# Rows of late stores shared unevenly among DMAs: from SyncE's queue to GpSimd's

## The chip, the cores and the metric

The kernel runs on one core of one Trainium2 chip. The metric is the device time of one execution in microseconds; of several runs the median is given. All times of the profile are from one execution that the hardware profiler recorded.

## The reference

For 8 batches of 12 heads, 512 positions and 64 dimensions, attention under a tree mask: position i sees itself and its ancestors (parent of i is (i-1)//2).

```python
mask = np.zeros((seq, seq))
for i in range(seq):
    mask[i, i] = 1
    parent = i
    while parent > 0:
        parent = (parent - 1) // 2
        mask[i, parent] = 1
scores = np.einsum('bhqd,bhkd->bhqk', Q, K) * scale + (1 - mask) * (-1e9)
weights = np.exp(scores - np.max(scores, axis=-1, keepdims=True))
weights = weights / (np.sum(weights, axis=-1, keepdims=True) + 1e-10)
return np.einsum('bhqk,bhkd->bhqd', weights, V).astype(np.float32)
```

Q, K, V and the output are float32, 12.58 MB each.

## The kernel before

The 96 heads are numbered through, two to a step, so there are 48 steps; from step 8 on two steps share a block of four heads, and `head(i, a)` gives the head of step i. A head's 512 positions lie on 128 partitions with four positions each, so a head is 1 KB of float32 on each partition.

All bulk loads are issued by GpSimd (POOL) and turn float32 into bfloat16 on the way; only the first two heads of Q and K come through SyncE (SP) and ScalarE. Per step, TensorE transposes K and Q, makes two sets of scores with the mask added as a product of code words, ScalarE takes the exponential into `e1` and `e2`, TensorE multiplies by the values with a column of ones, and VectorE (`norm`, lines 581 and 583) divides by the sum and writes the result into `of`, a float32 tile of 128 partitions for a group of eight heads. There are 11 such tiles in turn for the 12 groups.

Stores go out group by group. `store(eng, h0, n, step, p0, p1)` (line 590) issues one DMA on the queue of `eng` for n heads from h0 and for the partitions (rows) p0 to p1. The order on POOL is a list that `pool_program` writes out: loads, copies of V (`spread_pool`, `spread_top`) and stores. `pool(i)`, called at the end of each step, issues from the front of the list as long as `ready` says that what the front needs has been made. So an entry that is not ready holds back all behind it. In the loop over the last loads the store of group g is entered once the loads are BEHIND = 56 heads further; that places groups 0 to 4. What remains, groups 5 to 10, stands behind the last load and the last copies, with group 9 (heads 72 to 79) cut to its first four heads:

```python
for g in range(stored, NH // VO - 1):
    ops.append((store, nc.gpsimd, VO * g, APART - VO * g if g == APART // VO else VO))
```

Heads 76 to 79 are stored by `store_apart` in step 41 on SyncE's queue, in four DMAs over rows 0 to 63, 64 to 90, 91 to 115 and 116 to 127. Group 11 (heads 88 to 95) is stored in pieces, on SyncE's queue in the last three steps and, after the last step, one head each on SyncE's and ScalarE's queue.

Of the kernel before, what the change touches and what calls it, by code (L numbers as in the profile page):

```python
# [119 lines left out]
def kernel(  # L120
# [7 lines left out]
    nc = tc.nc  # L128
    B, H, S, D = Q.shape
    P = nc.NUM_PARTITIONS  # L130
    assert S == 512 and D == 64 and P == 128 and (B * H) % 4 == 0
    scale = float(1.0 / np.sqrt(D))
    NH = B * H
# [3 lines left out]
    KB, VB, VO = 8, 16, 8  # L137
# [126 lines left out]
    def head(i, a):  # L264

        return 2 * i + a if i < WIDE else 4 * (i // 2) + i % 2 + 2 * a
# [187 lines left out]
    def scores1(i):  # L454

        sp = psS.tile([P, 2, 512], fp32, name="s1")
        for a in range(2):
            nc.tensor.matmul(  # L458
                out=sp[:, a, :],
                lhsT=(k1code if i < WIDE else k1wide)[64 * a:64 * a + CODE_ROWS, :],  # L460
                rhs=(q1code[64 * a:64 * a + CODE_ROWS, :] if i < WIDE
                     else q1wide[64 * a:64 * a + CODE_ROWS, :, :]),
                start=True, stop=False,
            )
        for a in range(2):
            nc.tensor.matmul(  # L466
                out=sp[:, a, :], lhsT=keys(i, a, TOP),
                rhs=qTs[i][64 * a:64 * a + 64, :, :].rearrange("p t c -> p (t c)"),
                start=False, stop=True,
            )  # L470
        et = etpool.tile([P, 2, 4, 128], bf16, name="e1")
        nc.scalar.activation(  # L472
            out=et[:, :, :, :].rearrange("p a t c -> p (a t c)"),
            in_=sp[:, :, :].rearrange("p a c -> p (a c)"),
            func=AF.Exp, scale=scale,
        ) if i < WIDE else nc.scalar.activation(  # L476
            out=et[:, :, :, :].rearrange("p a t (r u) -> p a (t r) u", u=2),
            in_=sp[:, :, :].rearrange("p a (u c) -> p a c u", u=2),
            func=AF.Exp, scale=scale,
        )  # L480
        ets[i] = et
# [92 lines left out]
    def norm(i):  # L574
        g = head(i, 0) // VO
        if g not in ofs:
            ofs[g] = opool.tile([P, VO, 4, D], fp32, name="of")
        o4 = obs[i][:, :, 0:260].rearrange("p a (t c) -> p a t c", c=D + 1)
        rec = small.tile([P, 2, 4, 1], fp32, name="rec")
        for a, n in ((0, 2),) if i < NP - 1 else ((0, 1), (1, 1)):  # L580
            nc.vector.reciprocal(out=rec[:, a:a + n, :, :], in_=o4[:, a:a + n, :, D:D + 1])  # L581
            first, last, step = head(i, a) % VO, head(i, a + n - 1) % VO, head(i, 1) - head(i, 0)
            nc.vector.tensor_tensor(  # L583
                out=ofs[g][:, first:last + 1:step, :, :],
                in0=o4[:, a:a + n, :, 0:D],
                in1=rec[:, a:a + n, :, :].to_broadcast([P, n, 4, D]),
                op=ALU.mult,
            )

    def store(eng, h0, n, step=1, p0=0, p1=P):  # L590
        g, f = divmod(h0, VO)
        return eng.dma_start(  # L592
            out=Or[p0:p1, h0:h0 + step * (n - 1) + 1:step, :],
            in_=ofs[g][p0:p1, f:f + step * (n - 1) + 1:step, :, :].rearrange(
                "p h t d -> p h (t d)"
            ),
        )

    APART, APART_AT, APART_ROWS = 76, 41, (0, 64, 91, 116, P)

    def store_apart():

        for p0, p1 in zip(APART_ROWS, APART_ROWS[1:]):
            store(nc.sync, APART, 4, 1, p0, p1)

    def pool_program():

        ops = [
            (load_k, 2, 2), (load_q, 2, 2), (load_v, 0, 4), (load_v, 4, 4),
            (load_k, 4, 2), (load_k, 6, 2), (load_q, 4, 2), (load_k, 8, 4),  # L610
            (load_q, 6, 2), (load_q, 8, 4), (load_v, 8, 8), (load_k, 12, 4),
            (load_q, 12, 4), (load_k, 16, 4), (load_rows, 1, "upper"),
            (load_q, 16, 4), (load_rows, 1, "even"), (load_k, 20, 4), (load_rows, 1, "odd"),
            (load_q, 20, 4), (load_k, 24, 8), (load_q, 24, 4), (load_rows, 2, "upper"),
            (load_q, 28, 4), (load_k, 32, 4), (load_rows, 2, "even", "odd"),
            (load_q, 32, 8), (load_k, 36, 4), (load_rows, 3, "upper"),
            (spread_pool, (1, "Z0", 8, 16), (1, "Z1", 8, 16)),
            (load_k, 40, 8), (load_q, 40, 8), (load_rows, 3, "even", "odd"),
            (spread_top, 2, 0, 16), (spread_pool, (2, "Z0", 0, 16), (2, "Z1", 0, 16)),
            (load_q, 48, 4), (spread_pool, (2, "X", 0, 8)),  # L620
            (load_k, 48, 8), (spread_pool, (2, "X", 8, 16)),
            (load_q, 52, 4), (load_rows, 4, "upper"), (spread_top, 3, 0, 16),
            (load_k, 56, 8), (load_q, 56, 8), (load_rows, 4, "even", "odd"),
            (spread_pool, (3, "X", 0, 8), (3, "Z0", 0, 16), (3, "Z1", 0, 16), (3, "X", 8, 16)),
            (load_rows, 5, "upper"), (store, nc.gpsimd, 0, VO),
        ]
        loaded, stored = 88, 1
        for h in range(64, NH, KB):
            top = [(spread_top, h // VB + 0)] if h % VB == 8 and 4 <= h // VB + 0 < NH // VB else []
            ops += [(load_k, h, KB)] + top + [(load_q, h, KB)]  # L630
            while loaded < min(h + 32, NH):
                names = ("even", "odd") if loaded % VB else ("upper",)
                ops.append((load_rows, loaded // VB) + names)
                loaded += KB
            if top:
                o = h // VB
                ops.append((spread_pool, (o, "X", 0, 16), (o, "Z0", 0, 16), (o, "Z1", 0, 16)))
            while VO * stored + VO + BEHIND <= h + KB:
                ops.append((store, nc.gpsimd, VO * stored, VO))
                stored += 1  # L640
        for g in range(stored, NH // VO - 1):
            ops.append((store, nc.gpsimd, VO * g, APART - VO * g if g == APART // VO else VO))
        return ops

    def ready(op, i):

        f, args = op[0], op[1:]
        if f in (load_k, load_q):
            return 2 * (i + 3) >= args[0] + args[1] - 4 * KB
        if f is load_v:  # L650
            return True
        if f is load_rows:
            return 2 * i >= VB * (args[0] - 2)
        if f is spread_pool:
            tops = [(("vt", "M", VB * o + h) in issued) for o, part, h0, h1 in args if part == "X"
                    for h in range(h0, h1)]
            return 2 * i >= VB * (args[0][0] + 1 - NV) and all(tops)
        if f is spread_top:
            return 2 * i >= VB * (args[0] + 1 - NV)
        return 2 * i >= args[1] + args[2]  # L660

    BY_VECTOR = {
        0: [(0, 2, 0, 8), (0, 7, 0, 4), (0, 1, 0, 8), (0, 6, 0, 8), (0, 3, 0, 8), (0, 9, 0, 8)],
# [44 lines left out]
    def pool(i):  # L708
        while program and ready(program[0], i):
            op = program.pop(0)  # L710
            op[0](*op[1:])
# [18 lines left out]
    for i in range(NP + 1):  # L730
        steps = FIRST[i] if i < len(FIRST) else "SVK" if i % 2 else "SVQ"
        for step in steps:
            if step == "S" and i < NP:
                scores1(i)
                scores2(i)
            if step == "V" and i >= 1:
                values(i - 1)
                norm(i - 1)
                valued = True
            if step == "K" and kdone < NP:  # L740
                kdone = turn("kst", kdone)
            if step == "Q" and qdone < NP:
                qdone = turn("qst", qdone)
            if step == "W":
                nc.scalar.copy(
                    out=codes[64:64 + CODE_ROWS, 1280:1536], in_=codes[0:CODE_ROWS, 1280:1536]
                )
            if step == "X":
                spin("s1" if valued else "ob", 2)
            if step == "D":  # L750
                spread_by(nc.vector.tensor_copy, BY_VECTOR, STEADY_VECTOR, i)
            if step == "A":
                spread_by(nc.scalar.copy, BY_SCALAR, {}, i)
        if "D" not in steps:
            spread_by(nc.vector.tensor_copy, BY_VECTOR, STEADY_VECTOR, i)
        if "A" not in steps:
            spread_by(nc.scalar.copy, BY_SCALAR, {}, i)
        pool(i)
        if i == APART_AT:
            store_apart()  # L760
        if i >= NP - 3 and i < NP:
            store(nc.sync, head(i - 1, 0), 2, 2)
    assert not program
# [32 lines left out]
```

## Time and profile before

| | |
|---|---|
| runs | 134.94 us median of 3 (134.68 to 135.85) |
| profiled execution | 134.27 us, its span 132.4 us |
| busy in the span | PE 113.4, DVE 100.1, ACT 94.4, POOL 72.9 us |
| HBM | 37.94 MB read, 12.58 MB written |
| packets of GpSimd's queue (q0) | 29824, 29.63 MB |
| packets of SyncE's queue (q1) | 1836, 1.83 MB |
| packets of ScalarE's queue (q10) | 560, 0.46 MB |

The profile's DMA share is the time that packets took on the core's 16 DMA engines, divided by 16 engines' time; it can go a little over 1. GB/s counts the bytes as they are written, so that loads, which shrink on the way, show half the rate of stores. An issue is the instruction that hands a DMA to its queue; landing is when the last of its bytes is reported.

### The profile page before, as it was taken

What the parts mean: (1) busy time and instruction counts of PE and PEld (TensorE: products, weight loads), DVE (VectorE), ACT (ScalarE), POOL (GpSimd) and SP (SyncE); (2) the same over time, 40 slices, a digit from 0 to 9 for tenths busy, and PEclk for the clock granted to TensorE, in tenths of its full rate; (3) what the DMA queues carried; (4) which work ended last, traced back from release to release, by engine and by line L of the source; (5) the groups of instructions that cost most, each with busy time, mean ns of one, the idle gap of its engine ahead of it and who ended that gap; (6) DMA issues with size and microseconds to landing.
All of it is one profiled execution on the core that took longest, in us unless ns stands there. A gap on an engine that the chain in (4) does not pass through costs nothing.

```text
span 132.4 us, 5523 instructions
## 1 busy us (share of the span) xinstructions
PE 113.4 (86%) x2414; PEld 79.0 (60%) x2417; DVE 100.1 (76%) x249; ACT 94.4 (71%) x153; POOL 72.9 (55%) x100
## 2 busy tenths in 40 slices
PE   6886979999999899899989299999999997989800
PEld 2343755766676677676766276767666774756500
DVE  3539779889999999987965668899978896674620
ACT  4369577988888788778768455889796975969600
POOL 6999625454375999987732799437289600002000
PEclk9999999999999999999999958999999999999985
DMA  3999999999999999999999999999999999999992
GB/s 109 237 184 193 199 196 201 202 202 205 199 202 201 203 203 207 200 210 197 205 204 197 298 273 202 266 300 226 341 214 330 244 279 399 401 399 401 395 351 72
DMA packets 32244, 32.26 MB, mean 244 GB/s; under 512 B 1204, under 2 KB 29492, under 8 KB 32220
## 3 DMA queue, kind: packets, MB, share of 16 engines
q0 software_dynamic: 29824, 29.63, 114.7%
q1 hardware_dynamic: 1836, 1.83, 4.0%
q10 hardware_dynamic: 560, 0.46, 1.1%
q8 instruction: 19, 0.31, 0.9%
q14 instruction: 5, 0.04, 0.1%
HBM read 37.94 MB, written 12.58 MB: 382 GB/s over the span
## 4 chain that ended last, share of the span: by engine, by line
DMA 57%; PE 26%; POOL 5%; issue 4%; ACT 2%; DVE 1%; ACTq 0%; POOLq 0%
DMA vst<-in_V_dram 38%; DMA qst<-in_Q_dram 13%; PE ob L551 8%; DMA kst<-in_K_dram 7%; PE s L458 4%; PE s L466 3%; PE qtp L433 3%; PE ktp L401 2%; PE s L491 2%; PE s L501 2%; POOL vt L336 2%; POOL kst L251 1%; PE s L551 1%; ACT e L472 1%; ACT e L507 1%
## 5 line engine op out<-in xcount | busy, mean ns | idle before, releaser
L476 ACT ACTIVATE e<-s 128x1024 bf16<-128x1024 f32 x40 | 40.9, 1023 | 21.5 <-PE s L466 20.8
L551 PE MATMUL ob<-vt,e 128*128 128x65 bf16 (+1 forms) x940 | 38.0, 198 | 5.2 <-DVE of L583 3.8
L551 PEld LDWEIGHTS <-e 128*128 128x128 bf16 (+1 forms) x960 | 30.6, 103 | 13.7 <-DVE of L583 4.0
L507 ACT ACTIVATE e<-s 128x384 bf16<-128x384 f32 x80 | 34.7, 491 | 0.0
L583 DVE TENSOR_TENSOR of<-ob,rec 128x512 f32<-128x512 f32 x47 | 32.5, 691 | 1.6
L336 POOL COPY vt<-vst 32x512 int32<-32x512 int32 (+1 forms) x32 | 24.1, 754 | 7.2 <-DVE vt L336 3.9
L336 DVE COPY vt<-vst 64x1024 bf16<-64x1024 bf16 (+6 forms) x42 | 17.6, 420 | 5.7 <-DMA vst<-in_V_dram 5.1
L458 PE MATMUL s<-codes 40*128 40x512 bf16 x96 | 19.6, 395 | 1.2 <-issue 0.4
L581 DVE RECIPROCAL rec<-ob 128x8 f32<-128x8 f32 x47 | 9.7, 205 | 13.3 <-PE ob L551 12.7
L466 PE MATMUL s<-kq 64*128 64x512 bf16 x96 | 18.8, 382 | 0.0
L592 POOL DMA_DIRECT2D out_dram<-of x11 | 9.8, 895 | 15.5 <-DVE of L583 13.4
L280 POOL DMA_DIRECT2D vst<-in_V_dram x15 | 10.8, 723 | 12.7 <-DMA vst<-in_V_dram 7.0
L501 PEld LDWEIGHTS <-kq 64*128 64x128 bf16 x320 | 12.6, 95 | 4.7 <-issue 0.4
L501 PE MATMUL s<-kq 64*128 64x160 bf16 (+1 forms) x320 | 15.1, 210 | 0.0
L491 PE MATMUL s<-codes 40*128 40x384 bf16 x80 | 14.1, 339 | 0.1
L401 PE MATMUL ktp<-ptile,kst 128*64 128x128 bf16 x320 | 12.9, 224 | 1.2 <-issue 0.9
L441 DVE COPY kq<-qtp 128x1024 bf16<-128x1024 bf16 x20 | 13.6, 682 | 0.2 <-PE qtp L433 0.2
L433 PE MATMUL qtp<-ptile,qst 128*64 128x128 bf16 x320 | 12.7, 219 | 0.8 <-issue 0.7
L251 POOL DMA_DIRECT2D qst<-in_Q_dram x13 | 9.6, 738 | 5.1 <-DMA kst<-in_K_dram 1.7
L251 POOL DMA_DIRECT2D kst<-in_K_dram x12 | 9.1, 756 | 5.6 <-PE s L466 1.6
L491 PEld LDWEIGHTS <-codes 40*128 40x128 bf16 x80 | 6.4, 95 | 8.8 <-issue 1.1
L472 ACT ACTIVATE e<-s 128x1024 bf16<-128x1024 f32 x8 | 8.2, 1022 | 4.9 <-PE s L466 4.8
(42 smaller groups left out, 120.2 us busy)
## 6 DMA issues: line engine op xcount, KB each, us to landing
out_dram<-of POOLq DMA_DIRECT2D x10, 1024.0 KB, 16.3
kst<-in_K_dram POOLq DMA_DIRECT2D x8, 512.0 KB, 15.3
qst<-in_Q_dram POOLq DMA_DIRECT2D x7, 512.0 KB, 16.8
vst<-in_V_dram POOLq DMA_DIRECT2D x12, 256.0 KB, 14.1
vst<-in_V_dram POOLq DMA_DIRECT2D x6, 512.0 KB, 13.4
qst<-in_Q_dram POOLq DMA_DIRECT2D x8, 256.0 KB, 11.7
kst<-in_K_dram POOLq DMA_DIRECT2D x6, 256.0 KB, 11.7
out_dram<-of SPq DMA_DIRECT2D x4, 256.0 KB, 7.3
```

Of the source, the lines that this page charges most:

```text
L251: return nc.gpsimd.dma_start(out=kept[b][:, h0 % KB:h0 % KB + n, :, :].rearrange("p (g x) t d -> p g (x t d)", x=2), in_=wide[:, h0 // 2:( ...
L336: return copy(out=dst, in_=src)
L401: nc.tensor.transpose(out=columns(kp[64 * a:64 * a + 64, :], mixed, (256, 2), (leaves - mixed, 2), (1, 32)), in_=st[:, 2 * i % KB // 2 + a ...
L433: nc.tensor.transpose(out=halves[64 * a:64 * a + 64, :, c:c + 64], in_=st[:, 2 * i % KB // 2 + a, 4 * u + t, :], identity=ptile[:, 0:128],)
L458: nc.tensor.matmul(out=sp[:, a, :], lhsT=(k1code if i < WIDE else k1wide)[64 * a:64 * a + CODE_ROWS, :], rhs=(q1code[64 * a:64 * a + CODE_ ...
L466: nc.tensor.matmul(out=sp[:, a, :], lhsT=keys(i, a, TOP), rhs=qTs[i][64 * a:64 * a + 64, :, :].rearrange("p t c -> p (t c)"), start=False, ...
L476: ) if i < WIDE else nc.scalar.activation(
L491: nc.tensor.matmul(out=flat[:, a, :, :].rearrange("p u (t c) -> p u t c", t=4)[:, :, :, 16:64], lhsT=k2wide[64 * a:64 * a + CODE_ROWS, :], ...
L501: nc.tensor.matmul(out=flat[:, a, :, lo:hi], lhsT=keys(i, a, WTILE2[t]), rhs=qT[64 * a:64 * a + 64, :, lo:hi], start=False, stop=t == 1, s ...
L507: nc.scalar.activation(out=e2s[i % NE][:, a, :, 32:128].rearrange("p t (r u) -> p t r u", u=2), in_=flat[:, a, :, :].rearrange("p u (t r) ...
L551: nc.tensor.matmul(out=ob[lo:hi, a, 65 * t:65 * t + 65], lhsT=e[:, a, PLACE[t], lo:hi], rhs=vt[vtile[tile_v][0]][:, head(i, a) % VB, vtile ...
L583: nc.vector.tensor_tensor(out=ofs[g][:, first:last + 1:step, :, :], in0=o4[:, a:a + n, :, 0:D], in1=rec[:, a:a + n, :, :].to_broadcast([P, ...
```

## The change

SyncE's four stores of heads 76 to 79 go, and GpSimd stores group 9 (heads 72 to 79) in one DMA. Of the groups behind the last load, the first one is stored in pieces: its first two heads in six DMAs over 25, 2, 34, 6, 17 and 44 rows; then two whole groups; then its next four heads in four DMAs over 63, 7, 25 and 33 rows; then its last two heads in one DMA; then the remaining groups whole. By the counters of the code `stored` is 5 at this place, so the pieces are heads 40 and 41, 42 to 45, and 46 and 47; the whole groups between are 6 and 7, and those at the end 8, 9 and 10. `ready` rounds the end of a store up to a multiple of four heads, as a block of four is done together.

```diff
-    APART, APART_AT, APART_ROWS = 76, 41, (0, 64, 91, 116, P)
-
-    def store_apart():
-
-        for p0, p1 in zip(APART_ROWS, APART_ROWS[1:]):
-            store(nc.sync, APART, 4, 1, p0, p1)
+    PAIR_ROWS = (0, 25, 27, 61, 67, 84, P)
+    QUAD_ROWS = (0, 63, 70, 95, P)
...
-        for g in range(stored, NH // VO - 1):
-            ops.append((store, nc.gpsimd, VO * g, APART - VO * g if g == APART // VO else VO))
+        whole = list(range(stored + 1, NH // VO - 1))
+        for p0, p1 in zip(PAIR_ROWS, PAIR_ROWS[1:]):
+            ops.append((store, nc.gpsimd, VO * stored, 2, 1, p0, p1))
+        for g in whole[:2]:
+            ops.append((store, nc.gpsimd, VO * g, VO))
+        for p0, p1 in zip(QUAD_ROWS, QUAD_ROWS[1:]):
+            ops.append((store, nc.gpsimd, VO * stored + 2, 4, 1, p0, p1))
+        ops.append((store, nc.gpsimd, VO * stored + 6, 2))
+        for g in whole[2:]:
+            ops.append((store, nc.gpsimd, VO * g, VO))
         return ops
...
-        return 2 * i >= args[1] + args[2]
+        return 2 * i >= -(-(args[1] + args[2]) // 4) * 4
...
-        if i == APART_AT:
-            store_apart()
```

## The prediction

> **What bounds the kernel now.** I read the slices of the page first, then the share of the DMA engines by stage, then the last microseconds in steps of half a microsecond, then the issue times of the two queues that the change touches.
>
> ```profile
> span 132.4 us, 5523 instructions
> ...
> DMA  3999999999999999999999999999999999999992
> ...
> HBM read 37.94 MB, written 12.58 MB: 382 GB/s over the span
> ...
> DMA 57%; PE 26%; POOL 5%; issue 4%; ACT 2%; DVE 1%; ACTq 0%; POOLq 0%
> ```
>
> The 16 DMA engines are busy in every slice but the last, and the chain that ended last is mostly DMA. The profiled execution took 134.27 us, that is 1.9 around its span; the median of the runs is 134.94. I make the sum against the profiled 134.27 and carry the difference over to 134.94.
>
> By stage (columns: stretch and its length, busy time and count of PE, PEld, DVE, ACT, POOL, then granted clock, DMA share, GB/s; a share of 1.02 to 1.04 is what full engines show here, because packets overlap a little):
>
> ```profile
> 109.00:113.00 4.00, 3.09 (x74) 2.21 (x68) 2.58 (x6) 2.43 (x4) 0.00 (x0) 1.00 1.02 399
> 113.00:117.00 4.00, 4.00 (x100) 2.90 (x96) 2.95 (x7) 3.37 (x7) 0.00 (x0) 1.00 1.04 397
> 117.00:121.00 4.00, 3.43 (x73) 2.28 (x70) 2.69 (x7) 3.17 (x7) 0.90 (x1) 1.00 1.03 403
> 121.00:125.00 4.00, 3.98 (x80) 2.77 (x79) 1.73 (x5) 3.54 (x6) 0.00 (x0) 1.00 1.03 398
> ...
> 127.50:128.00 0.50, 0.00 (x0) 0.00 (x0) 0.00 (x0) 0.00 (x0) 0.00 (x0) 0.93 1.16 410
> 128.00:128.50 0.50, 0.00 (x0) 0.00 (x0) 0.00 (x0) 0.00 (x0) 0.00 (x0) 0.50 0.90 320
> 128.50:129.00 0.50, 0.00 (x0) 0.00 (x0) 0.00 (x0) 0.00 (x0) 0.00 (x0) 0.50 0.77 262
> 129.00:129.50 0.50, 0.00 (x0) 0.00 (x0) 0.00 (x0) 0.00 (x0) 0.00 (x0) 0.50 0.68 225
> 129.50:130.00 0.50, 0.00 (x0) 0.00 (x0) 0.00 (x0) 0.00 (x0) 0.00 (x0) 0.50 0.42 145
> 130.00:130.50 0.50, 0.00 (x0) 0.00 (x0) 0.00 (x0) 0.00 (x0) 0.00 (x0) 0.50 0.34 117
> 130.50:131.00 0.50, 0.00 (x0) 0.00 (x0) 0.00 (x0) 0.00 (x0) 0.00 (x0) 0.50 0.10 35
> 131.00:131.50 0.50, 0.00 (x0) 0.00 (x0) 0.00 (x0) 0.00 (x0) 0.00 (x0) 0.50 0.00 0
> ```
>
> From 109 to 128 the engines have no room at all. The change moves no byte in or out of the kernel, so this stretch can shrink only by cheaper packets. After 128 the share falls in steps: the engines do not finish together. Divided by the 1.03 of full engines, about 12 of the 16 are still busy at 128.5 to 129, 10 or 11 in the next half microsecond, 6 or 7 in the one after, 5 from 130 to 130.5. The shares from 128 to 131 sum to 3.21; times 0.5, over 1.03, that is 1.56 us of work in 3 us. Had it been spread evenly, the engines would have been done some 1.3 us before the last one (which ends near 130.9). **That 1.3 us is all that a perfect distribution could bring.** The slices of the last 3.4 us, each 0.085 us wide, show who is late:
>
> ```profile
> GB/s 253 241 241 217 205 181 193 181 145 121 121 120 121 121 121 120 121 84 84 48 24 12 0 0 0 0 0 0 0 0 0 0 0 0 0 0 0 0 0 0
> ...
> q1 hardware_dynamic: 194, 0.18, 15.5%
> ```
>
> A plateau of 121 GB/s against some 400 for 16 engines is five engines, late together by about 0.8 us.
>
> **The change, part by part.** The places on the queues, with start and time of the issues:
>
> ```profile
> 99.58 4.53 POOL L592 DMA_DIRECT2D out_dram<-of  x5
> 105.21 0.76 POOL L592 DMA_DIRECT2D out_dram<-of  x1 [1.09 <-DVE kq L441]
> 119.35 0.90 POOL L592 DMA_DIRECT2D out_dram<-of  x1 [13.38 <-DVE of L583]
> ...
> 109.03 17.87 SPq L592 DMA_DIRECT2D out_dram<-of  x8
> ...
> out_dram<-of POOLq DMA_DIRECT2D x6, 1024.0 KB, 16.6
> ```
>
> *POOL's issues.* Before, POOL issues groups 4 to 8 from 99.58, half of group 9 at 105.21, and group 10 at 119.35, after waiting 13.38 us for DVE. Afterwards there stand six, four and one partial stores in the place of group 5's single one: ten instructions more. From the five at 4.53 us one costs 0.91, from the shorter one 0.76; a piece with few rows may be cheaper, nothing excludes zero. So 0 to 9.1 us of POOL, and I take 8. Groups 4 to 8 are then out at 99.58 + 15 x 0.91 = 113.2 at the latest. Group 9 whole waits for heads 76 to 79, which SP's first of its four stores found ready at 109.03, so it goes out by about 114.1, still 5 us ahead of group 10. Nothing else stands behind on POOL (no spread, no load). The cover is the backlog of the queue: a store of 1 MB lands 16.6 us after its issue, so a piece that is issued 8 us later still finds its engine busy with earlier ones. Cost 0. Without that cover the whole 8 us would lie open, and this would show as a DMA share under 1 between 107 and 113.
>
> [...]
>
> *SyncE's four stores go.* They are 512 KB (rows 0 to 63, 64 to 90, 91 to 115, 116 to 127 of four heads) and now ride in POOL's whole store of group 9. SP has time before and after, its next store waits for DVE, cost 0. The packets differ:
>
> ```profile
> q0 software_dynamic: 312, 1.21, 101.7%
> ...
> q0 software_dynamic: 334, 1.29, 82.0%
> q1 hardware_dynamic: 288, 0.28, 20.1%
> ```
>
> The first row is 110 to 113, POOL's queue alone: 1.21 MB in 101.7% of 16 engines for 3 us, or 40.3 us of engine time per MB. The other two are 113 to 117 with SP's stores beside it: 0.28 MB in 20.1% of 4 us, or 46 us per MB. 512 KB less at 46 and more at 40.3 saves (0.524 x 5.7) / 16 = 0.19 us of every engine. The stage rows show less of a difference (399 GB/s alone, 397 to 403 mixed), which would give 0. I take **-0.1**.
>
> *Smaller runs.* Two heads instead of eight give 2 KB of a partition in place of 8 KB. The trace has no store of POOL in that shape. Between POOL's large packets (0) and SP's 1 KB packets for these 256 KB (0.262 x 5.7 / 16 = 0.09): I take **+0.05**.
>
> *Who gets how many rows.* This is the part that decides. SP's four stores of 64, 27, 25 and 12 rows are uneven over the engines, and so are the new ones: 25, 2, 34, 6, 17, 44 rows of 2 KB and 63, 7, 25, 33 rows of 4 KB, 768 KB in all or 48 KB for each engine on average. A row cannot be worth less than its run: 17 rows on 16 engines are at best 2 rows on one and 1 on the others, at worst all 17 (34 KB) on a single engine, 32 KB above its fair share. At 40.3 us per MB that engine is 1.3 us late. How the old unevenness stands to the engines' own speeds no view tells me; taking it out is worth between a gain of 1.3 us (all the tail is its doing) and a loss of 0.7 (it had been relieving the late ones: an engine that got only its four of the 64 rows has 16 KB instead of its fair 32, and 16 KB at 40.3 us per MB are 0.66 us). I take 0 for it, since a plateau of five can be read both ways. The new unevenness: from the steps of the tail about 6 of 16 engines have over 1.3 us to spare and swallow 32 KB unseen; some 4 have 0.9 and exceed the end by 0.4; the five late ones and the one near them exceed it by 1.0 to 1.3. The mean over them is (6 x 0 + 4 x 0.4 + 6 x 1.15) / 16 = +0.5. [...] I take **+0.4**, with bounds -1.3 and +2.0 (1.3 and 0.7 together).
>
> [...]
>
> The sum: -0.1 + 0.05 + 0.4 = +0.35; 134.27 becomes 134.6, and against the median 134.94 becomes **135.3**.
>
> **The rivals.**
>
> (1) *The heavy engine is a late one* (slower). [...] From the point where that engine has less than about 0.3 us to spare, its end moves by 1.0 to 1.3 us, and by up to 2.0 where the old stores had been relieving it. It gives 134.94 - 0.05 + 1.7 = 136.6. [...] Against it: row counts as odd as these look fitted to engines.
>
> (2) *The new rows fit the engines* (faster). [...] All of the tail's 1.3 us and the packets' 0.1 give 134.94 - 1.4 = 133.5. [...] Against it: everything must meet, and the heavy ones must fall on the four that end before 128.75.
>
> (3) *It doesn't do what it says*: POOL's queue hands rows to all 16 engines alike, or the distribution moves from run to run. Then only the old unevenness goes: 134.8, with single runs from 134 to 136.
>
> **How the numbers follow.** About 1% (1.35 us) is what a measurement of this kernel can tell from no change. The forecast with rival (3) is "within 1%": 0.52, likeliest time 135.3, its own range 134.0 to 136.2. Rival (1) has 0.36, from the bounds of the row term, whose upper end lies at +2.0 and whose lower at -1.3; the tail offers less to win than to lose. Rival (2) has 0.12: even a perfect spread is only just 1.0%. The range over all goes from 134.0, which leaves most of rival (2) out, to 136.9 (134.94 + 2.0), which takes all of rival (1) in.
>
> **What would show it.** Right: after the last load POOL shows sixteen issues, the ten added ones at 0.6 to 0.9 us each, all over by 115; the share stays near 1.02 from 109 to 127; SP has four issues, from 121 on; the tail is as long as before or longer, with a narrow plateau of one or two engines (25 to 50 GB/s) at its end. Wrong: a share that drops steeply from 1 to 0 within a microsecond of 129.9 (rival 2); a POOL issue well over 1 us, or a gap in the share before 120 (the cover failed); the old tail with five engines unchanged (rival 3 or the old unevenness never mattered).

## The result and the profile after

Six runs gave 137.15 us in the median (136.71 to 137.26), six of the kernel before 135.49 (134.68 to 136.08). The ratio is 1.0133, 95% interval 1.009 to 1.0176: **slower by 1.3%**, or 1.8 us by the ratio and 1.7 by the medians. The profiled execution took 137.2 us with a span of 135.4. The profiled execution of before (134.27) was one of its fastest, so the two traces differ by 3.0 us of span, more than the medians do.

The stages after the change, with the same columns as before:

```profile
109.00:113.00 4.00, 3.09 (x64) 1.99 (x60) 2.75 (x7) 2.25 (x5) 0.92 (x1) 1.00 0.92 311
113.00:117.00 4.00, 4.00 (x100) 2.93 (x96) 2.79 (x7) 3.42 (x6) 3.55 (x6) 1.00 0.97 373
117.00:121.00 4.00, 3.29 (x80) 2.46 (x77) 2.44 (x7) 2.86 (x5) 2.53 (x3) 1.00 0.88 271
121.00:125.00 4.00, 3.85 (x72) 2.47 (x71) 1.86 (x5) 3.82 (x8) 0.89 (x1) 1.00 1.02 386
```

Before, these four rows had a share of 1.02 to 1.04 and 397 to 403 GB/s. Now the share is short by 0.10, 0.07 and 0.15: over 4 us each, and divided by the 1.03 of full engines, **1.2 us in which the engines stood idle**. The bytes are short by more: against 399, 397, 403 and 398 GB/s before, 88, 24, 132 and 12 GB/s over 4 us are 1.02 MB, 2.6 us of work at 400 GB/s. So another 1.3 us went into packets that kept an engine busy without moving their bytes at the old rate: 271 GB/s at a share of 0.88 is 308 for a full share.

Who let the engines run dry stands in GpSimd's timeline after the last load (start, time, and in brackets the idle time before it and what ended it):

```profile
100.15 3.70 POOL L592 DMA_DIRECT2D out_dram<-of  x5
105.78 0.96 POOL L592 DMA_DIRECT2D out_dram<-of  x1 [1.93 <-DMA out_dram<-of]
108.13 0.64 POOL L592 DMA_DIRECT2D out_dram<-of  x1 [1.39 <-DMA kst<-in_K_dram]
110.67 0.92 POOL L592 DMA_DIRECT2D out_dram<-of  x1 [1.89 <-DMA qst<-in_Q_dram]
113.45 6.08 POOL L592 DMA_DIRECT2D out_dram<-of  x8 [1.87 <-DMA out_dram<-of]
121.39 0.89 POOL L592 DMA_DIRECT2D out_dram<-of  x1 [1.86 <-DVE rec L581]
```

A store needs nothing but its tile, and the tiles of groups 5 to 8 were long done. Yet GpSimd waits four times for landings, of a store, a load of K, a load of Q and a store again. In the trace the DMAs on GpSimd's queue signal on eight semaphores in turn (numbers 99 to 106), and each of these four issues follows 0.3 us after the landing of the DMA eight issues before. So eight can be under way, and at no time are there more. When six of the eight are pieces of 4 to 88 KB, hardly anything is left in the queue: when group 6 was issued at 110.67, the seven others that had not landed were 1.3 MB in all, 1.05 MB of it group 4, which was almost done. Group 7's issue at 113.45 waited for group 4 to land, and by then only group 6 and the end of the pieces lay before the engines.

This can explain the idle time up to 117, some 0.7 of the 1.2 us. From 117 to 121, where the share is lowest, it does not: five to eight DMAs, 1.6 to 3.9 MB, had been issued and not landed. Why engines stood idle there the trace does not tell.

The tail, in slices of 0.16 us from 129 to 135.4:

```profile
GB/s 454 390 378 384 378 346 359 365 384 378 365 365 346 352 333 269 237 262 218 179 102 96 96 90 83 51 51 45 45 38 13 0 0 0 0 0 0 0 0 0
```

The plateaus are now 96 (four engines) and 51 to 45 (two engines), and the last of the two ends 0.8 us after the four. The small packets also grew in number, from 1204 under 512 B before to 1778:

```profile
DMA packets 32442, 32.27 MB, mean 238 GB/s; under 512 B 1778, under 2 KB 29554, under 8 KB 32418
```

### The profile page after: what moved, and what is told of

The parts are those of the page before. It is cut to its first block, busy times and chain, and to the rows that moved or that the text cites. A ratio compares the mean times of both kernels' runs of the same rounds, so it can differ in the third digit from the quotient of the medians.

```text
span 135.4 us, 5528 instructions
## 1 busy us (share of the span) xinstructions
PE 113.8 (84%) x2417; PEld 79.0 (58%) x2417; DVE 99.4 (73%) x249; ACT 94.4 (70%) x153; POOL 79.7 (59%) x110
## 2 busy tenths in 40 slices
DMA packets 32442, 32.27 MB, mean 238 GB/s; under 512 B 1778, under 2 KB 29554, under 8 KB 32418
## 4 chain that ended last, share of the span: by engine, by line
DMA 52%; PE 25%; POOL 8%; issue 5%; ACT 2%; DVE 1%; ACTq 0%; POOLq 0%
DMA vst<-in_V_dram 40%; DMA qst<-in_Q_dram 13%; PE ob L551 8%; PE s L458 4%; PE s L466 3%; PE qtp L433 2%; PE ktp L401 2%; POOL kst L239 2%; POOL qst L239 2%; POOL vt L336 2%; PE s L491 2%; PE s L501 2%; POOL vst L239 1%; POOL kst L251 1%; ACT e L507 1%
## 5 line engine op out<-in xcount | busy, mean ns | idle before, releaser
L592 POOL DMA_DIRECT2D out_dram<-of x21 | 16.8, 804 | 9.9 <-DMA out_dram<-of 3.8
```

The source lines that it names most:

```text
L592: return eng.dma_start(out=Or[p0:p1, h0:h0 + step * (n - 1) + 1:step, :], in_=ofs[g][p0:p1, f:f + step * (n - 1) + 1:step, :, :].rearrange ...
```

## The experiments

The theories are named in the expectations: **L**, eight places on GpSimd's queue, so that small pieces run it dry; **R**, row counts that 16 does not divide (called odd here); and, formed after the first four runs, **P**, pieces of neighbouring rows, whose packets get in each other's way. A ratio is a run's time over that of the kernel before, taken beside it, with its 95% interval.

**e1_even.**

```diff
-    PAIR_ROWS = (0, 25, 27, 61, 67, 84, P)
-    QUAD_ROWS = (0, 63, 70, 95, P)
+    PAIR_ROWS = (0, 16, 32, 48, 64, 96, P)
+    QUAD_ROWS = (0, 32, 64, 96, P)
```

> The changed kernel with the rows of the pieces cut evenly (16, 16, 16, 16, 32, 32 and 32, 32, 32, 32), the same number of stores in the same places. Theory L (a store on GpSimd's queue waits until the DMA eight before it has landed, so small pieces use up the eight places and the queue runs dry): nothing of the loss comes back but the tail, 1.0 to 1.5 us slower than the kernel before, GpSimd still waits about 7 us for landings between 105 and 116, the DMA share still dips to 0.8 to 0.9 between 111 and 121. Theory R (row counts that 16 does not divide are cut into fragments and load the engines unevenly, packets get slower): within 0.4 us of the kernel before, and GB/s per share back at 390 to 400.

Ratio 1.0087 (1.0051 to 1.0124), 1.2 us slower. The waits of 2 us stay, as L has it, and the share falls to 0.90 between 109 and 113. But from 117 to 121 something is there that neither theory has: the engines are full and move 317 GB/s.

```profile
109.00:113.00 4.00, 3.09 (x70) 2.09 (x66) 2.75 (x7) 2.25 (x5) 0.97 (x2) 1.00 0.90 344
117.00:121.00 4.00, 3.79 (x83) 2.66 (x81) 3.09 (x8) 3.70 (x7) 2.45 (x3) 1.00 1.00 317
DMA packets 32010, 32.27 MB, mean 240 GB/s; under 512 B 1322, under 2 KB 29098, under 8 KB 31986
```

The packets under 512 B are 456 fewer than after the change, with as many DMAs. In the trace of after, 392 packets have 16 bytes and 64 have 8; e1_even has none of these sizes, so they come with the odd counts.

**e2_whole.**

```diff
-        whole = list(range(stored + 1, NH // VO - 1))
...
-        for g in whole[2:]:
+        for g in range(stored, NH // VO - 1):
             ops.append((store, nc.gpsimd, VO * g, VO))
```

> The changed kernel without any pieces: groups 5 to 10 whole on GpSimd's queue, nothing of group 9 on SyncE's. Both theories: no dip of the share between 109 and 127, no loss there. What it tells is the worth of SyncE's four uneven stores of before: if they held the late engines back by 0.7 us, this kernel is 0.5 to 0.7 us slower than before with a tail longer by that; if they did nothing or harm, it is level or up to 1 us faster. I expect 0 to +0.5 us.

Ratio 1.0019 (0.9984 to 1.0053): level with before. In time, SyncE's four uneven stores were worth nothing that this measurement can tell, and no share is lost up to 125 (1.02 to 1.05 in the four stages from 109). This kernel is the base for the pieces.

**e3_mixed.**

```diff
+        ops += pairs[0:2] + [w6] + pairs[2:3] + [w7] + pairs[3:5] + [w8, pairs[5], quads[0], w9]
+        ops += quads[1:4] + [(store, nc.gpsimd, VO * stored + 6, 2), w10]
```

`pairs` and `quads` are the lists of the pieces, `w6` to `w10` the stores of whole groups.

> The changed kernel with the same uneven pieces in the same order among themselves, but taken apart by the whole stores (two pieces, group 6, one piece, group 7, two pieces, group 8, one pair piece, one quad piece, group 9, three quad pieces, the last two heads, group 10), so that eight outstanding stores always hold 3 to 4 MB. Theory L: the dips of the share go, the time falls to within 0.5 us of the kernel before. Theory R: the share may be full, but GB/s per share stays at 290 to 350 while the pieces run, and 1.0 to 1.8 us of loss remain.

Ratio 1.0094 (1.0052 to 1.0136). The share is full again, and the loss of bytes stays:

```profile
109.00:113.00 4.00, 3.41 (x74) 2.26 (x71) 3.09 (x7) 2.57 (x6) 1.22 (x2) 1.00 1.05 386
117.00:121.00 4.00, 3.56 (x80) 2.51 (x75) 2.69 (x8) 3.18 (x6) 2.84 (x5) 1.00 1.02 355
121.00:125.00 4.00, 3.63 (x72) 2.33 (x69) 1.49 (x4) 3.81 (x7) 1.41 (x2) 1.00 1.00 342
```

The order alone takes away the idle time, as L has it. GpSimd still waits for landings (5.8 us in all), but with whole stores between the pieces enough is left in the queue. Without idle engines the kernel is still 1.3 us slower than before.

**e4_pieces.** The kernel before with the even pieces of e1_even for group 5, group 9 cut and SyncE's four stores kept.

> The kernel before, SyncE's four stores kept, with group 5 cut into ten even pieces and one of two heads at the places of the changed kernel. Theory L: 1.0 to 1.5 us slower than before, dips of the share after 109. Theory R: level with before (within 0.3 us).

Ratio 1.0128 (1.0074 to 1.0183), 1.7 us slower: even pieces at these places lose as much with SyncE's four stores beside them, with a share of 0.90 and 302 GB/s from 109 to 113, then 359 and 342 at a full share.

**e5_mixed_even.** The order of e3_mixed with the rows of e1_even.

> e3_mixed with the even rows of e1_even: both suspected costs taken away at once. If the loss is the sum of the eight places and of the odd row counts, this is level with e2_whole (within 0.4 us of the kernel before). Theory P (new: a piece with few rows is read by all 16 DMA engines from few partitions at once, its packets get in each other's way, however even the rows are): GB/s falls to 320 to 360 at a full share while the pieces run, packets of 4 KB take 300 to 700 ns instead of 165, and 0.6 to 1.0 us of loss stay.

Ratio 1.0014 (0.9982 to 1.0045): level, as the sum of L and R has it. P was wrong for this arrangement in its price (0.2 us slower than before, at most 0.6 by the interval, where it had 0.6 to 1.0). From 109 to 113 nothing is lost; from 121 to 125 bytes are short, which fits P, as the quad pieces are under way there:

```profile
109.00:113.00 4.00, 3.09 (x70) 2.09 (x66) 2.68 (x6) 2.57 (x6) 0.55 (x2) 1.00 1.04 400
121.00:125.00 4.00, 3.77 (x76) 2.42 (x70) 1.80 (x4) 3.82 (x8) 1.23 (x2) 1.00 0.98 356
```

**e6_heads.** Eleven pieces cut by heads, each with all 128 rows: `store(nc.gpsimd, h, 1)` for h from 40 to 45, groups 6 and 7, then 1 and 1 heads (46 and 47) and group 8 as 3, 3 and 2 heads.

> The changed kernel with its eleven pieces cut by heads instead of by rows: six stores of one head, two groups, five stores of 1, 1, 3, 3 and 2 heads, groups 9 and 10. Every piece has all 128 rows. Theory L (eight places): GpSimd still waits some 6 us for landings, with dips of the share to about 0.95 and 0.3 to 0.8 us lost (less than with e1_even, since a piece is larger). Theory P: no slow packets, GB/s per share 385 to 400 throughout.

Ratio 1.0023 (0.9991 to 1.0055). GpSimd waits as long for landings as in e1_even (7.8 us against 8.0), but six pieces of 128 KB keep more in the queue: the share falls only to 0.96 from 109 to 113. When the eighth store after the last load is issued, seven DMAs have not landed in each kernel, but they hold 1.3 MB in e1_even (share 0.90), 1.8 MB here (0.96) and 3.3 MB in e5_mixed_even (1.04). So a wait of GpSimd costs what it leaves the engines without, not what it lasts. The quiet packets that P expected don't hold throughout: 368 GB/s at a share of 1.00 from 117 to 121.

**e7_blocks and e8_stripes.** Both are e2_whole with groups 5 and 7 in four pieces of 32 rows; only the rows differ.

```python
ops.append((store, nc.gpsimd, VO * g, VO, 1, 32 * j, 32 * j + 32))  # e7: rows 32j to 32j+31
ops.append((store, nc.gpsimd, VO * g, VO, 1, j, P, 4))  # e8: rows j, j+4, j+8, ...
```

In e8_stripes `store` has a last argument, the step from row to row.

> e2_whole with groups 5 and 7 each stored in four blocks of 32 neighbouring rows (0 to 31, 32 to 63, and so on), 256 KB a piece; the eight places then hold at least 2.5 MB. Theory P: the 2 MB run at a full share but well below 390 GB/s, 1.5 to 4 us slower than before. Theory L: at most 0.5 us slower. Theory R: nothing, as 16 divides 32.

> e7_blocks with the same number, size and places of the pieces, but each piece takes every fourth row (0, 4, 8 and so on, then 1, 5, 9), so its 32 rows lie all over the partitions. Theory P: the loss of e7_blocks goes, GB/s back at 390 to 400 and within 0.5 us of e2_whole. Otherwise (what counts is the number or the size of the pieces): as slow as e7_blocks.

e7_blocks: 1.0234 (1.0186 to 1.0282), 3.2 us slower. e8_stripes: 1.0004 (0.9978 to 1.0031). The same number, size, places and waits, and 3 us apart. The stages of the two, e7_blocks first:

```profile
113.00:117.00 4.00, 4.00 (x102) 2.96 (x100) 2.79 (x7) 3.58 (x6) 2.68 (x4) 1.00 1.02 362
117.00:121.00 4.00, 3.56 (x84) 2.65 (x83) 2.72 (x8) 2.93 (x5) 0.89 (x1) 1.00 1.00 337
121.00:125.00 4.00, 3.63 (x67) 2.24 (x67) 1.68 (x4) 3.82 (x8) 0.00 (x0) 1.00 1.01 382
```

```profile
113.00:117.00 4.00, 4.00 (x102) 2.91 (x96) 2.78 (x8) 3.44 (x6) 2.85 (x4) 1.00 1.02 397
117.00:121.00 4.00, 3.56 (x84) 2.62 (x81) 2.69 (x8) 3.11 (x6) 0.89 (x1) 1.00 1.03 402
121.00:125.00 4.00, 3.79 (x74) 2.45 (x70) 1.86 (x5) 3.82 (x8) 0.00 (x0) 1.00 1.02 399
```

At an equal share of busy engines, neighbouring rows move 337 to 382 GB/s and scattered ones 397 to 402. The effect that P expected is shown; the loss is 9% and 16% in the first two rows. Why neighbouring rows move less no run here shows.

Not all of the 3 us is missing bytes. These rows lack 35, 65 and 17 GB/s over 4 us, 0.47 MB or 1.2 us at 400 GB/s. Behind them, TensorE stood still for 1.3 us in e7_blocks, until 126.10, and not in e8_stripes; e10_odd below has a likely reason.

**e9_bunched_stripes.** e1_even with scattered rows: pair pieces of every eighth (16 rows) or fourth row (32), quad pieces of every fourth.

> e1_even with the same sizes, number and places of the pieces, but every piece takes rows that lie all over the partitions (every eighth or fourth row). It leaves the eight places alone as a cost. Theory L: GpSimd waits for landings as in e1_even, the share dips to 0.9 between 109 and 113, no stretch with a full share under 380 GB/s; 0.3 to 0.7 us slower than e2_whole, between e2_whole and e1_even. If neighbouring rows were all of it: level with e2_whole.

Ratio 1.0097 (1.0063 to 1.0131), 1.3 us slower, as slow as e1_even. With the rows scattered the loss stays, so in the places of the change it does not come from neighbouring rows. (Four of the ten pieces take every eighth row, which no other run tries.) What is left is L, and it shows: the shares of 0.91 and 0.95 below are 0.7 us of idle engines. The price that I had put on it (0.3 to 0.7 us, measured 1.0 against e2_whole) was too low, and one stretch has a full share and few bytes all the same, 355 GB/s from 117 to 121, against the expectation:

```profile
109.00:113.00 4.00, 2.82 (x56) 1.84 (x58) 2.47 (x6) 2.14 (x4) 0.92 (x1) 1.00 0.91 344
113.00:117.00 4.00, 4.00 (x102) 2.98 (x97) 2.78 (x7) 3.54 (x6) 3.73 (x6) 1.00 0.95 374
117.00:121.00 4.00, 3.94 (x88) 2.78 (x84) 3.18 (x9) 3.37 (x7) 2.58 (x4) 1.00 1.00 355
```

What slows the packets after a starved stretch I did not settle; that part of the price belongs to the bunched places, but L does not explain it.

**e10_odd.** e2_whole with groups 5 and 7 in rows `0:126:2` (63), `1:128:2` (64) and row 126 alone.

> e2_whole with groups 5 and 7 each stored in three pieces that lie all over the partitions: rows 0, 2, 4 to 124 (63 rows), the 64 odd rows, and row 126 alone. Theory R (an odd number of rows costs by itself, in fragments or in uneven engines): some hundreds of packets under 512 B more than in e8_stripes, a longer tail, 0.3 to 0.8 us slower than e2_whole. If only neighbouring rows and the eight places count: within 0.3 us of e2_whole.

Ratio 1.0119 (1.0079 to 1.016). Scattered rows and few pieces, and still 1.4 us slower than e2_whole: odd counts cost time in few pieces and without blocks of neighbouring rows too. Packets under 512 B are 180 more than in e8_stripes (1438 against 1258).

By which way they cost it is less clear. In the profiled execution TensorE stood still for 2.3 us:

```profile
120.25 0.50 PE L551 MATMUL ob<-vt,e 128*128 128x65 bf16 x11 [2.27 <-issue]
```

The profile names no releaser, but its queue "instruction" does fit: it moves one packet of 16 KB about every 6 us, and in the thirteen traces each of the 36 stops of TensorE over 0.5 us without a releaser ends 2.2 to 2.7 us after the start of such a packet. In e10_odd that packet started at 117.98, 8.35 us after the one before (in e8_stripes 6.1 us). So TensorE very likely waited for its instructions, and their load came late; that the unevenly loaded engines delayed it is likely and not shown. The last store was then issued at 129.66 instead of 127.05 in e8_stripes, and the last packet of the stores ended 3.0 us after it instead of 4.3. So the longer tail that R expected is not what this trace shows.

**e11_probe17.** e2_whole with group 10 in 17, 96 and 15 rows.

> e2_whole with group 10 stored in three pieces, 17, 96 and 15 rows of 8 KB. It asks who carries 17 rows. If a single engine carries them: 136 KB on one engine, a tail with a plateau of 25 GB/s for 4 to 5 us and a span 3 to 5 us longer. If they are shared out in whole rows, 2 on eight engines and 1 on one: no plateau, span within 0.8 us of e2_whole. If they are cut into equal shares of bytes: no plateau either, and some 100 more packets under 512 B.

One run: 140.21 us, span 138.4 against 133.7 of e2_whole. The last 10.4 us in slices of 0.26 us:

```profile
GB/s 343 311 303 355 343 359 331 382 414 288 362 276 252 201 201 130 79 95 75 67 47 24 24 20 24 24 24 24 24 24 24 24 24 24 24 8 0 0 0 0
```

A plateau of 24 GB/s over fourteen slices, 3.6 us, at a share of 0.06 to 0.07, a sixteenth: one engine works alone, on 87 KB. That is the first case of the expectation, so **the seventeen rows very likely lie on a single engine**; which of the two small pieces the engine works on, the one of 17 rows or the one of 15, the rate alone does not show.

## Why the prediction was wrong

The direction of rival (1) came in, the forecast (within 1%, 135.3) and the range (to 136.9) did not. That rival (1)'s 136.6 lies near the measured 137.15 is partly luck: it has uneven engines in it, but no starved ones. 0.55 us of the miss is the base: the median of before went from 134.94 to 135.49 with three more runs.

*POOL's issues, cost 0: the step that failed.* I priced the issue times (8 us of POOL) and took the backlog of the queue as cover. The times were right, 0.57 to 0.97 us each. What I did not see is that the backlog is counted in DMAs, not in bytes, so the added pieces destroyed their own cover. The place was named (a share under 1 between 107 and 113), and it showed there. Two signs were off as well: 7 issues before and ten more are 17, not sixteen, and the added ones were over at 117.7 instead of 115. The cost: e1_even against e5_mixed_even, the same even pieces bunched and taken apart, is 0.87% against 0.14%, **about 1.0 us** by the difference of two ratios. About half of that is the share lost from 109 to 113 (0.90 against 1.04, 0.5 us); the rest is packets that moved fewer bytes afterwards, with the cause open. The count could have been read from the trace of before, where eight DMAs were under way at 105.21. There, GpSimd's waits (total, times, longest) are:

```profile
POOL vst L280 <- DMA vst<-in_V_dram: 7.0, 5, 2.5
POOL vst L280 <- DMA kst<-in_K_dram: 2.7, 3, 2.2
POOL vst L280 <- DMA qst<-in_Q_dram: 1.8, 1, 1.8
```

A load of V needs nothing of a load of K or Q. The semaphores of before show the shared count too: its 64 DMAs on GpSimd's queue take the same eight in turn.

*SyncE's four stores and the old unevenness, 0 with bounds -1.3 and +0.7: held.* e2_whole is at +0.19%, interval -0.16 to +0.53%.

*Cheaper and dearer packets, -0.1 and +0.05: not resolved* by any run; they are smaller than the intervals.

*The new unevenness, +0.4 with bounds -1.3 and +2.0: the right mechanism, sized too small.* e3_mixed against e5_mixed_even, odd against even rows in the same order, is 0.94% against 0.14%, **1.1 us**. No run shows by how much the lighter engines make up for the heavy ones, for which I went from +0.5 to +0.4; what the runs show in its place is this 1.1 us. The worst case that the term allowed, all 17 rows on one engine, is very likely what happens (e11_probe17, 24 GB/s for 3.6 us), and that the change ends with a narrow plateau was expected and is there. But part of these 1.1 us is not in the tail: the odd pieces move fewer bytes already from 117 to 125, at a full share (355 and 342 GB/s, the even ones 396 and 356). How the 1.1 us part between uneven engines, neighbouring rows and late instructions is open; e10_odd shows that odd counts cost without neighbouring rows, e7_blocks against e8_stripes that neighbouring rows cost without odd counts.

The two terms together would be 2.1 us on top of the base of e5_mixed_even (0.2), and the change measures 1.8: they overlap a little, or the intervals of 0.4% hide it. The sizes also depend on what is measured: 1.7 to 3.3 us of a run's time lie outside its span. By the medians of the spans alone, bunching costs 1.15 us (134.45 against 133.3) and odd counts 0.65 (133.95 against 133.3); with the 133.3 of e5_mixed_even that makes 135.1, and the change has 135.3. Rivals (2) and (3) are out: nothing got faster, and rows are not handed to all engines alike (one engine alone at the end of e11_probe17).

None of the eleven kernels beats the kernel before; e8_stripes, e5_mixed_even, e2_whole and e6_heads are level with it.

## What to carry to other kernels

Before cutting a transfer into pieces, look for what limits the number under way: an issue that waits for the landing of something it does not use tells of a shared count (eight DMAs here), and small pieces can then empty the queue that was meant to cover them (a share of 0.90 in e1_even, 1.04 in e5_mixed_even). In this kernel a piece of few rows does best with rows from all over the partitions (e7_blocks and e8_stripes differ in that alone and lie 3 us apart) and with a row count that 16 divides (e3_mixed and e5_mixed_even, about 1 us apart). Reshaping the loads of engines at the end can win only what the tail holds, 1.3 us here, and more than that was lost on the way.

## What the runs showed that I had not expected

Busy DMA engines can move 16% less: at a full share (1.00 and 1.03) the rate was 337 GB/s with neighbouring rows and 402 with scattered ones, so the share alone does not say that the engines work at their rate. Odd row counts bring packets of 8 and 16 bytes (1778 packets under 512 B against 1322 with the same number of even pieces). At the 9 to 11 ns that one took, the 456 are some 5 us of engine time, 0.3 us for each of 16 engines, so less than half of what odd counts cost. TensorE too seems to wait for the DMA engines now and then: its stops without a releaser end 2.2 to 2.7 us after the start of a packet of the instruction queue (a stop of 2.3 us in e10_odd).
